# Delta-rule gate projected with tokens on partitions, ahead of the mixer's other projections

## The chip, the cores and the metric

One Trainium2 chip, one of its cores. The metric is the device time of one execution in microseconds; the kernel before has a median of 1240.29 us over three runs (1238.09 to 1243.02).

## The reference, cut to what matters

Two networks follow each other on 256 tokens of width 1024. The first has a Mamba2 layer, an attention layer and two MLPs. The second, where the change lies, has a token mixer of two branches and a mixture of 32 experts. Inside the mixer:

```
proj = h @ w_in            # h is the normed, modulated input
qa, ka, va, qkv_b, z_b, b_b, a_b, gate_a, gate_b = split(proj)
y_a = attention(qa, ka, va)
qkv_b = silu(conv(qkv_b));  beta = sigmoid(b_b);  g = -exp(a_log) * softplus(a_b + dt_bias)
o_b = gated_delta_rule(q_b, k_b, v_b, beta, g)
y_b = rms_norm(o_b, onorm_w) * silu(z_b)          # z_b: 512 columns, the gate
m = sigmoid(gate_a) * (y_a @ w_up_a) + sigmoid(gate_b) * (y_b @ w_up_b)
return m @ w_out
```

## The kernel before, in words

Weights come from HBM as blocks of 128 x 2048 (`wload`, L187, through SyncE's queue into five `wraw` buffers). `split` (L196) cuts a block into two units of 1024 columns and turns each into a high part `whi` (ScalarE, L207) and a low part `wlo` (VectorE, or GpSimd for the units named in `pool`, L208). Both live in the pool `wsp`, which has as many buffers for each of the two as its argument says (L184); in the mixer that is 4, on the right end of SBUF (L909). A product is three matmuls, high x high, high x low, low x high (`mm3`, L235). All matmuls of such products have line L233.

Most projections have features on partitions: `fm` (L240) takes 128 weight columns as the stationary operand and 256 tokens as the moving one, so a block of 256 features is 48 matmuls of 256 columns. The attention values `va` have tokens on partitions: 128 tokens are stationary, 512 weight columns move, 24 matmuls for each of the two token halves (L936 to L942). The gate `z_b` is projected in the first way, two blocks of 256 features, and goes through `silu2` (L321: `th` on ScalarE, `zz` on VectorE).

The mixer's input `hT` is made in the stage before it: `rms_tile` (L880) norms one token half after the other, with its scratch tiles `dg` and `lv` in that stage's pool `mlp`. The last operation of each half is `hTl` (L904). The first half's `hT` is there some 9 us before the second's; the values' matmuls of the first token half stand in between. Every engine takes its instructions in the order that the planner gave them, which follows the order of the code, priorities and the planner's own estimate of when an operand is there.

`branches` (L922) is the mixer. The projections of its first part run in the order of `plan` (L989). From L1214 on a hand-written sequence of the delta rule runs, and `fill()` (L1185) puts units of independent matmuls between its steps: `fillers` (L1160) yields 28 of them, 4 for the gate (24 matmuls each), 16 for the two output gates (24 each) and 8 for `w_upa` (12 each). Between the sixteenth and the eight it loads two expert blocks early. The calls of `fill` from L1214 to L1281 take 24 units, and `fill(40)` (L1296) takes what is left. `dt_chain` (L960) computes the decay `g` and `beta` from `wba` (8 columns of weights, loaded at L944 through ScalarE's queue) and its split `w16`; its `ba` matmuls are the first after the values, and `sums` (L288) with the `csT` transposes follow later.

At the end of the delta rule (L1282 to L1295) the result `po` is scaled into `os_`, transposed (`ot`), multiplied by `onw` and the gate, and split into the two parts of `yb`, on which the `w_upb` products wait (L1299 to L1309, last step `mt` and `ml` on VectorE). Then `mixer_out` (L1312) loads a row `g1`, and SyncE's queue goes on to the expert weights `eraw` (L1537, 1 MB each), in order.

SBUF is laid out by pools, as the sizes in the code give it (bytes per partition). Pools that stay end at 72,320. In the first network `lnp` (17,088) and eight pairs of `wsp` (65,536) reach 154,944; `mlp` stands behind them, with 25,664 bytes of other tiles, then its two `lv` buffers at 180,608 to 184,704. In the mixer `keep` and `mixw` stand on the left and end at 181,760, and the four pairs of `wsp` take the right end from 196,576 to 229,344, `whi` below `wlo`.

Of the kernel before, what the change touches and what calls it, by code (L numbers as in the profile page):

```python
# [10 lines left out]
F32 = mybir.dt.float32  # L11
F32R = mybir.dt.float32r
# [6 lines left out]
T = 256  # L19
# [37 lines left out]
def lay(i):  # L57
# [67 lines left out]
    for n in ("q", "k"):  # L125
# [15 lines left out]
                                                    ("z", 3072, 512), ("g", 3592, 2048))}  # L141
    for n, c in cols.items():
        a["w_b" + n] = fblocks(w, c)
    a["w_bva"] = kblocks(w[:, 1024:1536])
    ba = np.concatenate([w[:, 3588:3592], w[:, 3584:3588]], axis=1)
# [14 lines left out]
def build(tc, A, out, dbg=None):  # L160
# [3 lines left out]
    with ctx:  # L164
# [123 lines left out]
        def sums(work, bank, n, da, ncs, rs):  # L288
            p = bank("cs")
            mm(p[:, 0:n], ic, da[:, 0:n], True, True)  # L290
            mm(p[:, n:2 * n], iu, da[:, n:2 * n], True, True)
            mm(p[:, 2 * n:3 * n], ic, da[:, n:2 * n], True, True)
            mm(p[:, 3 * n:4 * n], su, da[:, 0:n], True, True)
            cs = p[:, 0:3 * n].rearrange("p (b n) -> p b n", b=3)
            csr = work.tile([128, 3, n], F32, name="csr", tag="th")
            V.tensor_copy(csr, cs)
            V.tensor_scalar(ncs, cs[:, 0:3:2], -1.0, None, op0=OP.mult)
            V.tensor_copy(rs, p[:, 3 * n:4 * n])
            p = bank("csT")
            for b in range(3):  # L300
                PE.transpose(p[:n, b * 128:b * 128 + 128], csr[:, b], ident)
            row = work.tile([n, 384], F32, name="csrow", tag="cbm", bufs=2 if n == 32 else 1)
            V.tensor_copy(row, p[:n, 0:384])
            nc.scalar.dma_start(csd[n], row)
# [602 lines left out]
        def phase_mixer(keep, hT):  # L907
            gates = [keep.tile([128, 8, T], F32, name="gates", tag=t) for t in ("gA", "gB")]
            with wsp_pool(4, "right") as w_:  # L909
# [12 lines left out]
        def branches(keep, work, psm, hT, gates):  # L922
# [6 lines left out]
            for tag, n, bufs in (("va", 1024, 1), ("pt", 384, 4), ("s", 384, 3), ("lm", 896, 1), ("cbm", 384, 1), ("bc", 1536, 1), ("ml0", 512, 1),  # L929
                                 ("ml1", 512, 1), ("MT", 1536, 1), ("PT", 1536, 1), ("Tn0", 512, 1), ("Tn1", 512, 1),  # L930
                                 ("X0", 512, 1), ("X1", 512, 1), ("zz", 1024, 1), ("bias", 2048, 1), ("QK", 2048, 1)):
                work.tile([128, n], F32, name=tag, tag=tag, bufs=bufs)
            va = work.tile([128, 2, 512], F32, name="va", tag="va")
            vacc = [pa("va") for _ in range(2)]
            hls = [wsplit(A["w_bva"][b], pool=(0, 1)) for b in range(2)]
            for m in range(2):  # L936
                ms = slice(m * 128, m * 128 + 128)
                for c in range(8):
                    hl = hls[c // 4]
                    wh, wl = (x[:, (c % 2) * 512:(c % 2) * 512 + 512] for x in hl[c % 4 // 2])  # L940
                    mm3(vacc[m], hT[0][:, c, ms], hT[1][:, c, ms], wh, wl, c == 0, c == 7)
                S.activation(va[:, m], vacc[m], AF.Copy)  # L942
            wba = work.tile([128, 8, 8], F32, name="wba", tag="wba")
            nc.scalar.dma_start(wba, A["w_bba"])  # L944
# [11 lines left out]
            w16 = work.tile([128, 8, 16], F32R, name="w16", tag="w16")  # L956
            S.activation(w16[:, :, 0:8], wba, AF.Copy)
            V.tensor_tensor(w16[:, :, 8:16], wba, w16[:, :, 0:8], op=OP.subtract)
# [25 lines left out]
            zz = work.tile([128, 4, T], F32, name="zz", tag="zz")  # L984
# [175 lines left out]
            def fillers():  # L1160
                for b in range(2):
                    for f, p in enumerate(proj2("w_bz", b)):
                        silu2(work, p, zz[:, 2 * b + f])
                        yield
# [86 lines left out]
            def values(b):  # L1251
# [8 lines left out]
                for h in range(4):  # L1260
                    junk = work.tile([128, 128], F32, name="junk", tag="jk", bufs=2)
# [22 lines left out]
            ybt = zz  # L1284
            for b in range(2):
                os_ = work.tile([128, 4, 128], F32, name="os_", tag=f"X{b}")
                V.tensor_tensor(os_, v4(po[b]), ss[:, 1, 4 * b:4 * b + 4].unsqueeze(2).to_broadcast([128, 4, 128]),
                                op=OP.mult)
                p = pa("ot")
# [3 lines left out]
                V.scalar_tensor_tensor(ybt[:, :, bs], v4(p), onw[:, 0:1], zz[:, :, bs], op0=OP.mult, op1=OP.mult)  # L1293
                S.activation(yb[0][:, :, bs], ybt[:, :, bs], AF.Copy)
                V.tensor_tensor(yb[1][:, :, bs], ybt[:, :, bs], yb[0][:, :, bs], op=OP.subtract)  # L1295
# [557 lines left out]
```

## Time and profile before

| | |
|---|---|
| median of three runs | 1240.29 us |
| the profiled execution | 1241.94 us |
| its span, first to last instruction | 1240.2 us |
| mean granted TensorE clock | 0.983 |
| TensorE matmul busy | 1181.6 us (95%) |
| VectorE / ScalarE / GpSimd busy | 757.1 / 554.4 / 215.7 us |

The profile is of one execution. Times in its rows are counted from the first instruction. PE is TensorE's matmul, PEld its weight load, DVE VectorE, ACT ScalarE, POOL GpSimd, SP SyncE; "q" behind an engine is its queue of DMA issues. The granted clock is a share of full speed; 0.50 is 1.2 GHz, 1.00 is 2.4 GHz. The duration of a pipelined matmul overlaps that of the next, so the distance of two starts says what one costs.

### The profile page before, as it was taken

The page shows a single profiled execution, that of the slowest core. Times are in us where ns is not written, and L with a number is a line of the kernel's source. Part 1 is how long each engine was busy: PE and PEld are TensorE (multiplying, and loading weights), DVE is VectorE, ACT ScalarE, POOL GpSimd, SP SyncE. Part 2 cuts the span into 40 slices and gives each one's busy share as a digit, 9 for nine tenths or more (in the row PEclk, how much of TensorE's full clock was granted, in tenths as well). Part 3 has the DMA queues.
Part 4 walks back from the last instruction along what each step waited for, and adds up shares of the span by engine and source line. Part 5 has one row for each costly group of instructions (what it writes and reads, how often), then busy time and mean ns, then how long its engine had stood idle before and what let it go on. Part 6 is the DMA issues. An engine that isn't in the chain of part 4 may idle for free. (4 is left out here: it accounts for less than half of the span.)

```text
span 1240.2 us, 19177 instructions
## 1 busy us (share of the span) xinstructions
PE 1181.6 (95%) x7669; PEld 966.7 (78%) x7669; DVE 757.1 (61%) x1241; ACT 554.4 (45%) x910; POOL 215.7 (17%) x164
## 2 busy tenths in 40 slices
PE   8799996999999999999999998999999989999995
PEld 7799995889899889978999987998999853444332
DVE  5878877497777675559777766667455772111113
ACT  4577573354444455646544434554444431111112
POOL 3355543000000000000000043355431020000001
PEclk9899999999999999999999999899999999999998
DMA  8655634547887744324878753443325599999992
GB/s 325 220 187 196 221 128 146 206 175 282 311 312 285 253 170 170 137 101 158 330 282 300 276 201 118 163 170 103 103 69 204 232 388 407 421 422 421 421 421 108
DMA packets 47078, 295.84 MB, mean 239 GB/s; under 512 B 5256, under 2 KB 6533, under 8 KB 14469
## 3 DMA queue, kind: packets, MB, share of 16 engines
q1 hardware_dynamic: 41120, 277.91, 59.6%
q10 hardware_dynamic: 5860, 16.63, 3.9%
q8 instruction: 62, 1.02, 0.3%
q14 instruction: 36, 0.29, 0.1%
HBM read 293.38 MB, written 2.71 MB: 239 GB/s over the span
## 5 line engine op out<-in xcount | busy, mean ns | idle before, releaser
L208 DVE TENSOR_TENSOR wlo<-wraw,whi 128x1024 fp32r<-128x1024 f32 x240 | 303.1, 1278 | 146.4 <-ACT whi L207 145.5
L207 ACT ACTIVATE whi<-wraw 128x1024 fp32r<-128x1024 f32 x282 | 294.0, 1057 | 212.0 <-PE acc L233 65.4
L208 POOL TENSOR_TENSOR wlo<-wraw,whi 128x1024 fp32r<-128x1024 f32 x42 | 109.8, 2622 | 265.6 <-ACT whi L207 265.6
L233 PE MATMUL u<-hTh,whi 128*128 128x256 f32 x448 | 125.7, 281 | 0.0
L233 PE MATMUL u<-hTh,wlo 128*128 128x256 f32 x448 | 125.3, 280 | 0.0
L233 PE MATMUL u<-hTl,whi 128*128 128x256 f32 x448 | 125.2, 280 | 0.0
L233 PE MATMUL pj<-xh,whi 128*128 128x256 f32 x384 | 113.2, 295 | 6.4 <-ACT whi L387 5.3
L233 PE MATMUL gu<-eraw,xg 128*64 128x512 f32 x512 | 113.3, 595 | 1.1 <-PE xgp L233 0.6
L233 PE MATMUL acc<-whi,mh 128*128 128x512 f32 x288 | 113.8, 395 | 0.0
L233 PE MATMUL pj<-xh,wlo 128*128 128x256 f32 x384 | 110.6, 288 | 3.3 <-DVE wlo L208 3.2
L233 PE MATMUL acc<-whi,ml 128*128 128x512 f32 x288 | 112.7, 391 | 0.0
L233 PE MATMUL acc<-wlo,mh 128*128 128x512 f32 x288 | 112.3, 390 | 0.0
L233 PE MATMUL pj<-xl,whi 128*128 128x256 f32 x384 | 110.8, 289 | 0.3
L233 PE MATMUL pj<-hTh,whi 128*128 128x256 f32 x320 | 93.4, 292 | 0.0
L233 PE MATMUL pj<-hTh,wlo 128*128 128x256 f32 x320 | 91.1, 285 | 0.0
L233 PE MATMUL pj<-hTl,whi 128*128 128x256 f32 x320 | 91.0, 284 | 0.0
L233 PEld LDWEIGHTS gu<-eraw,xg 128*64 128x64 f32 x512 | 36.9, 137 | 66.7 <-issue 62.5
L233 PEld LDWEIGHTS u<-hTh,whi 128*128 128x128 f32 x448 | 84.1, 188 | 1.7 <-issue 0.6
L233 PEld LDWEIGHTS u<-hTl,whi 128*128 128x128 f32 x448 | 83.9, 187 | 1.1
L233 PEld LDWEIGHTS u<-hTh,wlo 128*128 128x128 f32 x448 | 84.4, 188 | 0.0
L233 PEld LDWEIGHTS pj<-xh,whi 128*128 128x128 f32 x384 | 75.3, 196 | 8.8 <-ACT whi L387 5.3
L233 PEld LDWEIGHTS pj<-xh,wlo 128*128 128x128 f32 x384 | 75.5, 197 | 3.9 <-DVE wlo L208 3.4
(450 smaller groups left out, 2386.6 us busy)
## 6 DMA issues: line engine op xcount, KB each, us to landing
wraw<-in_w_dram SPq DMA_DIRECT2D x64, 1024.0 KB, 5.0
eraw<-in_w_gu_dram SPq DMA_DIRECT2D x58, 1024.0 KB, 19.3
eraw<-in_w_dn_dram SPq DMA_DIRECT2D x30, 1024.0 KB, 19.8
wraw<-in_w_mod_dram SPq DMA_DIRECT2D x24, 1024.0 KB, 6.0
wraw<-in_w_a_dram SPq DMA_DIRECT2D x23, 1024.0 KB, 5.3
wraw<-in_w_ao_dram SPq DMA_DIRECT2D x8, 1024.0 KB, 5.0
wraw<-in_w_bg_dram SPq DMA_DIRECT2D x8, 1024.0 KB, 5.1
bc<-csd ACTq DMA_DIRECT2D x16, 384.0 KB, 5.7
```

Of the source, the lines that this page charges most:

```text
L207: his.append(S.activation(h, r[:, us], AF.Copy).ins)
L208: (G if u in pool else V).tensor_tensor(l, r[:, us], h, op=OP.subtract)
L233: return PE.matmul(o, a, b, start=start, stop=stop, skip_group_check=True).ins
```

## The change

The gate's weights get the layout of the values' weights, and its projection moves to the top of `branches`, with tokens on partitions: for each token half the first four of eight weight chunks right behind that half's values, and the last four of both halves after that. `silu2` runs there on token-major rows, so `zz` is [128, 2, 512] from then on. The pool of split weights has 6 pairs instead of 4; to make room `csrow` shares the tag `s`, and `junk` has one buffer. `wba` is loaded first, through SyncE's queue, and `w16` is made between the values' halves. The gate's four units leave `fillers`. At the end, `os_` is multiplied by the gate before the transposes, and `yb` comes straight from the transposed tile.

```
@@ -138,10 +138,11 @@
     a["rel"] = f(i["rel_bias_2"])
     w = f(i["w_in_2"])[0]
     cols = {n: range(c, c + k, 256) for n, c, k in (("qa", 0, 512), ("ka", 512, 512), ("qkv", 1536, 1536),
-                                                    ("z", 3072, 512), ("g", 3592, 2048))}
+                                                    ("g", 3592, 2048))}
     for n, c in cols.items():
         a["w_b" + n] = fblocks(w, c)
     a["w_bva"] = kblocks(w[:, 1024:1536])
+    a["w_bz"] = kblocks(w[:, 3072:3584])
     ba = np.concatenate([w[:, 3588:3592], w[:, 3584:3588]], axis=1)
     a["w_bba"] = np.ascontiguousarray(ba.reshape(8, 128, 8).transpose(1, 0, 2))
     for n in "ab":
@@ -299,7 +300,7 @@
             p = bank("csT")
             for b in range(3):
                 PE.transpose(p[:n, b * 128:b * 128 + 128], csr[:, b], ident)
-            row = work.tile([n, 384], F32, name="csrow", tag="cbm", bufs=2 if n == 32 else 1)
+            row = work.tile([n, 384], F32, name="csrow", tag="cbm" if n == 32 else "s", bufs=2 if n == 32 else 3)
             V.tensor_copy(row, p[:n, 0:384])
             nc.scalar.dma_start(csd[n], row)
 
@@ -906,7 +907,7 @@
 
         def phase_mixer(keep, hT):
             gates = [keep.tile([128, 8, T], F32, name="gates", tag=t) for t in ("gA", "gB")]
-            with wsp_pool(4, "right") as w_:
+            with wsp_pool(6, "right") as w_:
                 wsp_box.append(w_)
                 with tc.tile_pool(name="mixw", bufs=1, reuse_waits="tile") as work, \
                         tc.tile_pool(name="psm", bufs=4, space=PSUM, reuse_waits="tile") as psm:
@@ -926,22 +927,41 @@
             def v4(p):
                 return p.rearrange("p (h n) -> p h n", h=4)
 
-            for tag, n, bufs in (("va", 1024, 1), ("pt", 384, 4), ("s", 384, 3), ("lm", 896, 1), ("cbm", 384, 1), ("bc", 1536, 1), ("ml0", 512, 1),
+            for tag, n, bufs in (("va", 1024, 1), ("pt", 384, 4), ("s", 384, 3), ("lm", 896, 1), ("bc", 1536, 1), ("ml0", 512, 1),
                                  ("ml1", 512, 1), ("MT", 1536, 1), ("PT", 1536, 1), ("Tn0", 512, 1), ("Tn1", 512, 1),
                                  ("X0", 512, 1), ("X1", 512, 1), ("zz", 1024, 1), ("bias", 2048, 1), ("QK", 2048, 1)):
                 work.tile([128, n], F32, name=tag, tag=tag, bufs=bufs)
+            wba = work.tile([128, 8, 8], F32, name="wba", tag="wba")
+            nc.sync.dma_start(wba, A["w_bba"])
+            w16 = work.tile([128, 8, 16], F32R, name="w16", tag="w16")
             va = work.tile([128, 2, 512], F32, name="va", tag="va")
-            vacc = [pa("va") for _ in range(2)]
-            hls = [wsplit(A["w_bva"][b], pool=(0, 1)) for b in range(2)]
+            zz = work.tile([128, 2, 512], F32, name="zz", tag="zz")
+
+            def rows_in(p, hls, m, cs=range(8)):
+                ms = slice(m * 128, m * 128 + 128)
+                for c in cs:
+                    wh, wl = (x[:, (c % 2) * 512:(c % 2) * 512 + 512] for x in hls[c // 4][c % 4 // 2])
+                    mm3(p, hT[0][:, c, ms], hT[1][:, c, ms], wh, wl, c == 0, c == 7)
+
+            def silu_rows(p, m):
+                for n in range(2):
+                    silu2(work, p[:, n * 256:n * 256 + 256], zz[:, m, n * 256:n * 256 + 256])
+
+            hva = [wsplit(A["w_bva"][b], pool=(0, 1)) for b in range(2)]
+            pva, pz = ([pa(n) for _ in range(2)] for n in ("va", "z"))
+            rows_in(pva[0], hva, 0)
+            S.activation(va[:, 0], pva[0], AF.Copy)
+            hz = [wsplit(A["w_bz"][0], pool=(0, 1))]
+            rows_in(pz[0], hz, 0, range(4))
+            S.activation(w16[:, :, 0:8], wba, AF.Copy)
+            V.tensor_tensor(w16[:, :, 8:16], wba, w16[:, :, 0:8], op=OP.subtract)
+            rows_in(pva[1], hva, 1)
+            S.activation(va[:, 1], pva[1], AF.Copy)
+            hz.append(wsplit(A["w_bz"][1], pool=(1,)))
+            rows_in(pz[1], hz, 1, range(4))
             for m in range(2):
-                ms = slice(m * 128, m * 128 + 128)
-                for c in range(8):
-                    hl = hls[c // 4]
-                    wh, wl = (x[:, (c % 2) * 512:(c % 2) * 512 + 512] for x in hl[c % 4 // 2])
-                    mm3(vacc[m], hT[0][:, c, ms], hT[1][:, c, ms], wh, wl, c == 0, c == 7)
-                S.activation(va[:, m], vacc[m], AF.Copy)
-            wba = work.tile([128, 8, 8], F32, name="wba", tag="wba")
-            nc.scalar.dma_start(wba, A["w_bba"])
+                rows_in(pz[m], hz, m, range(4, 8))
+                silu_rows(pz[m], m)
             lm = work.tile([128, 7, 128], F32, name="lm", tag="lm")
             nc.scalar.dma_start(lm, A["lvl"])
 
@@ -953,9 +973,6 @@
             beta = work.tile([128, 2, 4], F32, name="beta", tag="beta")
             onw = work.tile([128, 1], F32, name="onw", tag="onw")
             V.tensor_scalar(onw, P("onw"), 0.5, None, op0=OP.mult)
-            w16 = work.tile([128, 8, 16], F32R, name="w16", tag="w16")
-            S.activation(w16[:, :, 0:8], wba, AF.Copy)
-            V.tensor_tensor(w16[:, :, 8:16], wba, w16[:, :, 0:8], op=OP.subtract)
 
             def dt_chain():
                 p = pst("ba")
@@ -981,7 +998,6 @@
             QK = work.tile([128, 8, T], F32, name="QK", tag="QK")
             vT = keep.tile([128, 2, 2, 4, 128], F32, name="vT", tag="vT")
             vt = vT[:, 0]
-            zz = work.tile([128, 4, T], F32, name="zz", tag="zz")
             qk = keep.tile([128, 2, 4, T], F32, name="qk", tag="qk")
             qa, ka = qk[:, 0], qk[:, 1]
 
@@ -1158,10 +1174,6 @@
             early = []
 
             def fillers():
-                for b in range(2):
-                    for f, p in enumerate(proj2("w_bz", b)):
-                        silu2(work, p, zz[:, 2 * b + f])
-                        yield
                 for b in range(8):
                     for f, p in enumerate(proj2("w_bg", b)):
                         S.activation(gates[b // 4][:, 2 * b % 8 + f], p, AF.Tanh, scale=0.5)
@@ -1258,7 +1270,7 @@
                         mm(o, PT[:, h, 128:256], w[0][:, h], True, False)
                         mm(o, PT[:, h, 256:384], w[1][:, h], False, True)
                 for h in range(4):
-                    junk = work.tile([128, 128], F32, name="junk", tag="jk", bufs=2)
+                    junk = work.tile([128, 128], F32, name="junk", tag="jk", bufs=1)
                     S.activation(junk, v4(po[b])[:, h], AF.Square, accum_out=ss[:, 0, 4 * b + h:4 * b + h + 1])
                 r = slice(4 * b, 4 * b + 4)
                 V.tensor_scalar(ss[:, 1, r], ss[:, 0, r], 1.0 / 128, 1e-6, op0=OP.mult, op1=OP.add)
@@ -1281,18 +1293,18 @@
             fill(2)
             yb2 = keep.tile([128, 2, 4, T], F32R, name="yb", tag="vT")
             yb = [yb2[:, d] for d in range(2)]
-            ybt = zz
             for b in range(2):
                 os_ = work.tile([128, 4, 128], F32, name="os_", tag=f"X{b}")
                 V.tensor_tensor(os_, v4(po[b]), ss[:, 1, 4 * b:4 * b + 4].unsqueeze(2).to_broadcast([128, 4, 128]),
                                 op=OP.mult)
+                V.tensor_tensor(os_, os_, zz[:, b].rearrange("p (h n) -> p h n", h=4), op=OP.mult)
                 p = pa("ot")
                 for h in range(4):
                     PE.transpose(v4(p)[:, h], os_[:, h], ident)
                 bs = slice(b * 128, b * 128 + 128)
-                V.scalar_tensor_tensor(ybt[:, :, bs], v4(p), onw[:, 0:1], zz[:, :, bs], op0=OP.mult, op1=OP.mult)
-                S.activation(yb[0][:, :, bs], ybt[:, :, bs], AF.Copy)
-                V.tensor_tensor(yb[1][:, :, bs], ybt[:, :, bs], yb[0][:, :, bs], op=OP.subtract)
+                S.activation(yb[0][:, :, bs], v4(p), AF.Copy, scale=onw[:, 0:1])
+                V.scalar_tensor_tensor(yb[1][:, :, bs], v4(p), onw[:, 0:1], yb[0][:, :, bs],
+                                       op0=OP.mult, op1=OP.subtract)
             fill(40)
             mh = keep.tile([128, 8, T], F32R, name="mh", tag="gA")
             ml = keep.tile([128, 8, T], F32R, name="ml", tag="qk")
```

## Rows read from the trace of the kernel before

**Rows 1.** The page, busy tenths in 40 equal slices of the span, TensorE and its granted clock

```profile
PE   8799996999999999999999998999999989999995
...
PEclk9899999999999999999999999899999999999998
```

**Rows 2.** Chain of waits (start us, us, what), SyncE's waits, SyncE's timeline

```profile
1100.13 17.20 DMA eraw<-in_w_gu_dram
...
SPq L524 <- DVE mt L1307: 16.2, 1, 16.2
...
973.42 9.58 SPq L1537 DMA_DIRECT2D eraw<-in_w_gu_dram  x10
```

**Rows 3.** Windows: us, busy (x) of PE, PEld, DVE, ACT, POOL; PEclk, DMA share, GB/s

```profile
860.00:945.00 85.00, 85.00 (x732) 81.53 (x731) 42.17 (x93) 39.60 (x93) 31.98 (x17) 1.00 0.26 88
...
1100.00:1200.00 100.00, 98.05 (x458) 38.32 (x458) 16.73 (x31) 12.99 (x27) 1.18 (x2) 0.99 1.01 421
```

**Rows 4.** Timeline of TensorE, 740 to 764 us; in brackets idle before <- releaser

```profile
743.71 0.39 PE L233 MATMUL va<-whi,hTh 128*128 128x512 f32 x1
...
751.32 2.05 PE L233 MATMUL tp<-dg,h 128*128 128x128 f32 x16 [0.97 <-DVE dg L883]
754.40 0.50 PE L233 MATMUL va<-whi,hTh 128*128 128x512 f32 x1 [1.03 <-DVE hTh L901]
...
761.62 0.29 PE L233 MATMUL ba<-hTh,w 128*16 128x256 f32 x1 [1.09 <-DVE w L958]
```

**Rows 5.** The same timeline, first and last of 21 and of 90 products

```profile
755.46 0.40 PE L233 MATMUL va<-whi,hTh 128*128 128x512 f32 x1
...
760.14 0.40 PE L233 MATMUL va<-whi,hTl 128*128 128x512 f32 x1
...
764.62 0.28 PE L233 MATMUL pj<-hTh,whi 128*128 128x256 f32 x1
...
775.18 0.28 PE L233 MATMUL pj<-hTh,wlo 128*128 128x256 f32 x1
```

**Rows 6.** Timelines of VectorE, ScalarE and GpSimd, 700 to 805 us

```profile
755.66 0.69 DVE L904 TENSOR_TENSOR hTl<-lv,hTh 128x512 fp32r<-128x512 f32 x1 [0.60 <-ACT hTh L903]
...
716.64 4.84 ACT L207 ACTIVATE whi<-wraw 128x1024 fp32r<-128x1024 f32 x5
...
717.76 9.11 POOL L208 TENSOR_TENSOR wlo<-wraw,whi 128x1024 fp32r<-128x1024 f32 x3 [2.25 <-ACT whi L207]
...
802.67 2.43 POOL L208 TENSOR_TENSOR wlo<-wraw,whi 128x1024 fp32r<-128x1024 f32 x1 [8.12 <-ACT whi L207]
```

**Rows 7.** TensorE's timeline at 790 and 200 us, and a window between

```profile
790.48 0.49 PE L301 MATMUL csT<-ident,csr 128*4 128x128 f32 x3 [2.51 <-DVE csr L296]
...
792.00:797.00 5.00, 5.00 (x25) 5.00 (x25) 0.00 (x0) 0.10 (x1) 2.37 (x1) 0.50 0.29 72
...
199.95 0.61 PE L233 MATMUL ss<-ones,Zg 128*128 128x1 f32 x4 [3.44 <-POOL Zg L479]
...
201.25 0.63 PE L233 MATMUL acc<-wlo,yh 128*128 128x512 f32 x1
201.68 0.63 PE L233 MATMUL acc<-whi,yl 128*128 128x512 f32 x1
```

**Rows 8.** End of the delta rule: TensorE, VectorE, ScalarE, 953 to 960 us

```profile
953.34 0.66 PE L1291 MATMUL ot<-ident,os__9610 128*128 128x128 f32 x4
...
953.86 1.40 DVE L1293 SCALAR_TENSOR_TENSOR zz<-ot,onw,zz 128x512 f32<-128x512 f32 x2
955.18 1.22 DVE L208 TENSOR_TENSOR wlo<-wraw,whi 128x1024 fp32r<-128x1024 f32 x1
956.31 1.28 DVE L1295 TENSOR_TENSOR yb<-zz,yb 128x512 fp32r<-128x512 f32 x2
...
954.63 1.29 ACT L1294 ACTIVATE yb<-zz 128x512 fp32r<-128x512 f32 x2 [0.80 <-DVE zz L1293]
...
959.46 0.40 PE L233 MATMUL up<-yb,whi 128*128 128x256 f32 x2
```

More of the change, by code (lines that the diff above doesn't have):

```diff
@@ L144, in lay @@
     a["w_bva"] = kblocks(w[:, 1024:1536])
+    a["w_bz"] = kblocks(w[:, 3072:3584])
     ba = np.concatenate([w[:, 3588:3592], w[:, 3584:3588]], axis=1)
@@ L301, in sums @@
                 PE.transpose(p[:n, b * 128:b * 128 + 128], csr[:, b], ident)
-            row = work.tile([n, 384], F32, name="csrow", tag="cbm", bufs=2 if n == 32 else 1)
+            row = work.tile([n, 384], F32, name="csrow", tag="cbm" if n == 32 else "s", bufs=2 if n == 32 else 3)
             V.tensor_copy(row, p[:n, 0:384])
@@ L908, in phase_mixer @@
             gates = [keep.tile([128, 8, T], F32, name="gates", tag=t) for t in ("gA", "gB")]
-            with wsp_pool(4, "right") as w_:
+            with wsp_pool(6, "right") as w_:
                 wsp_box.append(w_)
@@ L927, in v4 @@
                 return p.rearrange("p (h n) -> p h n", h=4)
-            for tag, n, bufs in (("va", 1024, 1), ("pt", 384, 4), ("s", 384, 3), ("lm", 896, 1), ("cbm", 384, 1), ("bc", 1536, 1), ("ml0", 512, 1),
+            for tag, n, bufs in (("va", 1024, 1), ("pt", 384, 4), ("s", 384, 3), ("lm", 896, 1), ("bc", 1536, 1), ("ml0", 512, 1),
                                  ("ml1", 512, 1), ("MT", 1536, 1), ("PT", 1536, 1), ("Tn0", 512, 1), ("Tn1", 512, 1),
@@ L932, in branches, with rows_in, silu_rows @@
                 work.tile([128, n], F32, name=tag, tag=tag, bufs=bufs)
+            wba = work.tile([128, 8, 8], F32, name="wba", tag="wba")
+            nc.sync.dma_start(wba, A["w_bba"])
+            w16 = work.tile([128, 8, 16], F32R, name="w16", tag="w16")
             va = work.tile([128, 2, 512], F32, name="va", tag="va")
-            vacc = [pa("va") for _ in range(2)]
-            hls = [wsplit(A["w_bva"][b], pool=(0, 1)) for b in range(2)]
-            for m in range(2):
[L937 to L944, printed above, removed]
+            zz = work.tile([128, 2, 512], F32, name="zz", tag="zz")
+            def rows_in(p, hls, m, cs=range(8)):
+                ms = slice(m * 128, m * 128 + 128)
+                for c in cs:
+                    wh, wl = (x[:, (c % 2) * 512:(c % 2) * 512 + 512] for x in hls[c // 4][c % 4 // 2])
+                    mm3(p, hT[0][:, c, ms], hT[1][:, c, ms], wh, wl, c == 0, c == 7)
+            def silu_rows(p, m):
+                for n in range(2):
+                    silu2(work, p[:, n * 256:n * 256 + 256], zz[:, m, n * 256:n * 256 + 256])
+            hva = [wsplit(A["w_bva"][b], pool=(0, 1)) for b in range(2)]
+            pva, pz = ([pa(n) for _ in range(2)] for n in ("va", "z"))
+            rows_in(pva[0], hva, 0)
+            S.activation(va[:, 0], pva[0], AF.Copy)
+            hz = [wsplit(A["w_bz"][0], pool=(0, 1))]
+            rows_in(pz[0], hz, 0, range(4))
+            S.activation(w16[:, :, 0:8], wba, AF.Copy)
+            V.tensor_tensor(w16[:, :, 8:16], wba, w16[:, :, 0:8], op=OP.subtract)
+            rows_in(pva[1], hva, 1)
+            S.activation(va[:, 1], pva[1], AF.Copy)
+            hz.append(wsplit(A["w_bz"][1], pool=(1,)))
+            rows_in(pz[1], hz, 1, range(4))
+            for m in range(2):
+                rows_in(pz[m], hz, m, range(4, 8))
+                silu_rows(pz[m], m)
             lm = work.tile([128, 7, 128], F32, name="lm", tag="lm")
@@ L955, in branches @@
             V.tensor_scalar(onw, P("onw"), 0.5, None, op0=OP.mult)
-            w16 = work.tile([128, 8, 16], F32R, name="w16", tag="w16")
-            S.activation(w16[:, :, 0:8], wba, AF.Copy)
-            V.tensor_tensor(w16[:, :, 8:16], wba, w16[:, :, 0:8], op=OP.subtract)
             def dt_chain():
@@ L983, in branches @@
             vt = vT[:, 0]
-            zz = work.tile([128, 4, T], F32, name="zz", tag="zz")
             qk = keep.tile([128, 2, 4, T], F32, name="qk", tag="qk")
@@ L1160, in fillers @@
             def fillers():
[L1161 to L1164, printed above, removed]
                 for b in range(8):
@@ L1260, in values @@
                 for h in range(4):
-                    junk = work.tile([128, 128], F32, name="junk", tag="jk", bufs=2)
+                    junk = work.tile([128, 128], F32, name="junk", tag="jk", bufs=1)
                     S.activation(junk, v4(po[b])[:, h], AF.Square, accum_out=ss[:, 0, 4 * b + h:4 * b + h + 1])
@@ L1288, in branches @@
                                 op=OP.mult)
+                V.tensor_tensor(os_, os_, zz[:, b].rearrange("p (h n) -> p h n", h=4), op=OP.mult)
                 p = pa("ot")
@@ L1292, in branches @@
                 bs = slice(b * 128, b * 128 + 128)
-                V.scalar_tensor_tensor(ybt[:, :, bs], v4(p), onw[:, 0:1], zz[:, :, bs], op0=OP.mult, op1=OP.mult)
-                S.activation(yb[0][:, :, bs], ybt[:, :, bs], AF.Copy)
-                V.tensor_tensor(yb[1][:, :, bs], ybt[:, :, bs], yb[0][:, :, bs], op=OP.subtract)
+                S.activation(yb[0][:, :, bs], v4(p), AF.Copy, scale=onw[:, 0:1])
+                V.scalar_tensor_tensor(yb[1][:, :, bs], v4(p), onw[:, 0:1], yb[0][:, :, bs],
+                                       op0=OP.mult, op1=OP.subtract)
             fill(40)
```

3 lines of the change are left out of this document (1 added, 2 removed).

## The prediction

> **What bounds the kernel now.** I read the page first. TensorE is busy in nearly every slice and its clock dips only where it idled [rows 1]. The end, though, is not TensorE's: from 1100 us the chain of waits is one expert weight load after another, and the DMA share there is 1.01 [rows 2, 3]. So the loads end the run, and their start is the question. The SyncE timeline has the first ten of them at 973.42 us, right behind the gate row `g1`, for which SyncE waited 16.2 us, until the mixer's last `mt` operation had let go of the bytes `g1` gets [rows 2]. Two things follow: whatever moves the end of the mixer moves the end of the kernel one for one, and a tile of a new pool waits for the last reader of the old tile in its bytes. From 860 to 945 us TensorE is busy 85.00 of 85 us [rows 3], so work taken away there is time won, while holes nearer 750 us are the ones the change means to fill: 0.97 us before the norm's `tp` matmuls, 1.03 us behind them, 1.09 us before `ba`, 3.1 us together [rows 4].
>
> **The change, part by part.**
>
> **The matmuls.** The gate needs 96 matmuls of 256 columns today, and 48 of 512 after. At 512 columns 21 rows start between 755.46 and 760.14 us, (760.14 - 755.46) / 20 = 0.234 us apart; at 256 columns 90 rows between 764.62 and 775.18, 10.56 / 89 = 0.119 us apart [rows 5]. So 48 x 0.234 = 11.2 us go in near 750 us and 96 x 0.119 = 11.4 us leave the stretch behind 820 us: -0.2 us. The wider form wins nothing, it only moves. The Trainium skill, page "TensorE: Matmul & The Clock Gate", section "Back-to-back issue gap", gives a sustained 131 ns per matmul at 512 columns; by that the 48 would cost 6.3 us and my total would be 4.9 us lower, but the rows show 0.234 us and decide.
>
> **The splits, where this goes wrong.** To hold the gate's weights beside the values', the pool of split weights goes from four pairs to six and grows downwards by 16,384 bytes. By the tile sizes in the code it then begins at byte 180,192, with `whi` lowest. The previous stage's `lv` tiles, the scratch of the norm, lie at 180,608 to 184,704. The lowest `whi` buffer and 416 bytes of the next overlap them; with four pairs (from 196,576) nothing did. The last reader of `lv` is VectorE's `hTl` of the second token half, 755.66 + 0.69 = 756.35 us [rows 6]. Today the values' four `whi` are made from 716.6 us and their `wlo` by 726.9, long before the norm ends [rows 6]. I take it that the first `whi` gets the lowest buffer and that later tiles of the same tag are not handed out past it; no row shows the second point, so it carries a chance below. Then no split of this stage starts before 756.35. The first matmul needs one `whi` (4.84 / 5 = 0.97 us) and one GpSimd `wlo` (2.43 alone, 3.04 in a run [rows 6]): 756.35 + 0.97 + 2.43 = 759.8, with hand-overs 760.
>
> TensorE meanwhile: today the values start at 743.7 [rows 4] and fill the norm. After, it idles from 743.7 to `tp` at 751.3, 7.6 us; from the end of `tp`, 753.4, to 760 it has only `ba` (16 matmuls of 256 columns, 16 x 0.119 = 1.9 us), 4.7 us idle. New idle 12.3 us against 3.1 us now: **+9.2 us**. What is behind the waiting instruction: on ScalarE the five other `whi`, on GpSimd their `wlo`, on TensorE all of the mixer.
>
> From 760 on a unit of 1,024 weight columns feeds 12 matmuls (both token halves), 12 x 0.234 = 2.8 us, and GpSimd gives one each 2.4 to 3.0 us. If the halves interleave it hides: 0 us, else up to 3 us. The gate's second block puts one `wlo` on VectorE and one on GpSimd, beside matmuls: 0.
>
> **The clock.** After 3.44 us of idle, matmuls of 512 columns start 0.43 us apart instead of 0.234; after the 2.51 us before `csT` the granted clock is 0.50, the 1.2 GHz level, for all of 792 to 797 us [rows 7]. Two idles of 7.6 and 4.7 us bring the same twice: `tp` (2.05 us [rows 4]) takes 0.43 / 0.234 = 1.84 times as long, +1.7 us on the norm's own path; and `ba` with the first eight or so value matmuls loses 8 x 0.2 = 1.6 us. **+3.3 us**, bounds 0 (the clock stays) and 5.
>
> **The fillers.** 28 units cover the waits of the delta rule today; without the gate's four there are 24, and the calls ahead of `fill(40)` are exactly 24. So nothing is left behind the `ot` transposes, where four units of 12 matmuls (5.6 us) cover the way to `yb` now: `ot` at 953.34, ScalarE 954.63, VectorE 956.31, first matmul on `yb` 959.46 [rows 8]. That way gets a multiplication by the gate more (0.64 us, like the subtraction 1.28 / 2 [rows 8]). TensorE, done with `ot` at 953.9, waits until about 956.5, 2.6 us, and `up` on `ya` now follows attention at once, 0.4 more: **+3 us**. Bounds 0, and 5 if both 1.22 us weight subtractions stand in front on VectorE [rows 8].
>
> **Small moves.** The gate's four `th`/`zz` pairs of 256 columns move forward, under matmuls: 0; without that cover at most 0.7 us each on VectorE, what 512 columns take [rows 8], 2.8 us. `wba` goes from ScalarE's queue to SyncE's; what is behind it there are loads whose buffers are full until splits start: 0. The two gate loads pass in front of the projections' on SyncE; those are needed 20 us later than now: 0. `csrow` in an `s` buffer, one `junk` buffer (ScalarE is in order anyway), the new `yb` pair (one operation for one): 0.
>
> **A stall that may go.** Before `csT` TensorE waits 2.51 us for VectorE, and the half clock behind it costs 5 x (1 - 0.234 / 0.43) = 2.3 us [rows 7]. With splits made during the gate's matmuls VectorE may be ahead there: between -4.8 and 0; nearer to neither, I take **-2.4**.
>
> Sum: -0.2 + 9.2 + 0 + 3.3 + 3 - 2.4 = **+12.9 us**. The profiled execution took 1241.94 us (span 1240.2 and 1.74 around it), 1.65 above the median of the runs, 1240.29. 1241.94 + 12.9 - 1.65 = **1253.2 us**. With each bound: +9.2 - 0.2 - 4.8 = +4.2 at best, 9.2 - 0.2 + 3 + 5 + 5 = +22 at worst: 1244.5 to 1262.3.
>
> **The rivals.** *The buffers come free in time* (0.16), the case that is not slower: no overlap counts, or the planner gives the blocked buffer to a later tile. Then 12 gate matmuls (2.8 us) fill two norm holes (-2.0), `ba` waits no more (-1.1), the end still loses 3 and the stall half goes: -0.2 - 3.1 + 3 - 2.4 = -2.7, 1237.6 us; with the bounds 1232 to 1244. For it: ScalarE and GpSimd are free around 725 us. Against: the bytes. It decides from where the first `whi` starts: before 743 us it holds.
>
> *Only the first buffer is held* (0.08): five splits are made early, but matmuls accumulate from the first unit, so the values still wait until 760; only the gate's 12 matmuls (2.8 us) run in the norm. 12.9 - 2.8 = +10.1: 1250.4 us.
>
> *GpSimd in the norm's way* (0.06): buffers free, but the gate's two subtractions (2.4 to 3.0 us each) stand before a power operation of the norm on GpSimd, worth up to 5 us: -2.7 + 5 = +2.3, 1242.6 us. Against: GpSimd idles from 726.9.
>
> **The numbers.** My forecast holds 0.70. Some 0.5% (6.2 us) is what a measurement of this kernel can tell from no change: below 1234.1 faster, above 1246.5 slower. Slower: nearly all of the forecast (0.66) and of the second rival (0.07): 0.73. Within: tails of these (0.05), over half of the first rival (0.09), the third (0.05): 0.19. Faster: the rest of the first rival, 0.08. 1240 to 1260 takes in the forecast but for its tails, the second and third rivals and the upper part of the first: some 0.8. The likeliest case alone is 1244.5 to 1262.3.
>
> **What would show it.** Right: the first `whi` of the values behind `hTl`, after 756 us, no matmul on `va` before `tp`, idle in front of `tp` near 7 us, granted clock 0.50 near 760, projections starting near 785 instead of 763.5, TensorE waiting for `yb` at the end, and the first expert loads some 13 us later. Wrong: `whi` near 717 us and matmuls on `z` between 750 and 755 us.

## The result and the profile after

The changed kernel is slower: 1255.1 us median (1252.77 to 1259.78, six runs) beside 1239.19 us (1236.3 to 1243.53, six runs), a ratio of 1.0129 with a 95% interval of 1.0102 to 1.0156. The forecast was 1253.2 us, the range 1240 to 1260. A ratio in this document compares fast executions alone and is estimated apart from the two medians beside it, so it can differ from their quotient by some 0.2%. The profiled execution is the slowest of the six, 1259.78 us, with a span of 1258.1 us and a mean granted clock of 0.975.

The two profiled executions do not reach the mixer at the same moment: the norm's first `tp` starts at 738.66 us, before at 740.5. So the stage is compared from there. From the first `tp` to the end of the span the kernel before takes 1240.2 - 740.5 = 499.7 us, this one 1258.1 - 738.7 = 519.4 us: 19.7 us more.

The page's busy tenths in 40 slices, TensorE and its granted clock, the counterpart of [rows 1]:

```profile
PE   8799987999999999999999968999999989999995
PEclk9899998999999999999999988999999979999998
```

Slice 24, from 723 to 755 us, was at 9 tenths or more before and is down to 6 tenths; the clock dips in it and in the next. The timeline of ScalarE at the end of the norm shows why:

```profile
754.92 0.63 ACT L904 ACTIVATE hTh<-lv 128x512 fp32r<-128x512 f32 x1
...
756.36 1.06 ACT L208 ACTIVATE whi<-wraw 128x1024 fp32r<-128x1024 f32 x1 [0.71 <-issue]
...
757.32 4.83 ACT L208 ACTIVATE whi<-wraw 128x1024 fp32r<-128x1024 f32 x5
```

VectorE's timeline has the last reader of `lv` right before it:

```profile
755.58 0.69 DVE L905 TENSOR_TENSOR hTl<-lv,hTh 128x512 fp32r<-128x512 f32 x1 [1.41 <-ACT hTh L904]
```

`hTl` ends at 755.58 + 0.69 = 756.27 and the first `whi` starts at 756.36; before, the values' `whi` came from 716.64 on [rows 6]. TensorE's timeline over the norm, the counterpart of [rows 4, 5] (a figure in brackets is the idle time before the row and what ended it):

```profile
749.50 3.78 PE L234 MATMUL tp<-dg,h 128*128 128x128 f32 x16 [7.43 <-DVE dg L884]
757.47 0.79 PE L234 MATMUL va<-whi,hTh 128*128 128x512 f32 x1 [4.18 <-ACT whi L208]
759.90 0.79 PE L234 MATMUL va<-wlo,hTh 128*128 128x512 f32 x1 [1.64 <-POOL wlo L209]
760.49 0.63 PE L234 MATMUL va<-whi,hTl 128*128 128x512 f32 x1
760.92 0.63 PE L234 MATMUL va<-whi,hTh 128*128 128x512 f32 x1
...
764.12 0.39 PE L234 MATMUL va<-whi,hTl 128*128 128x512 f32 x1
764.35 0.40 PE L234 MATMUL va<-whi,hTh 128*128 128x512 f32 x1
...
771.63 0.50 PE L234 MATMUL z<-wlo,hTh 128*128 128x512 f32 x1 [0.67 <-POOL wlo L209]
```

No matmul on `va` or `z` stands between the two `tp` rows of the norm, and four waits take 7.43 + 4.18 + 1.64 + 0.67 = 13.9 us. `tp` takes 3.78 us where it took 2.05, and the values begin 0.43 us apart (760.49, 760.92) and only later 0.23 (764.12, 764.35). The projections start at 787.3 us, 48.6 us behind the first `tp`; before it was 763.5 - 740.5 = 23.0.

At the other end of the mixer, the counterpart of [rows 8]:

```profile
971.03 0.60 PE L1303 MATMUL ot<-ident,os__9615 128*128 128x128 f32 x4
972.80 0.65 PE L1303 MATMUL ot<-ident,os__9625 128*128 128x128 f32 x4 [1.17 <-DVE os__9625 L1300]
974.24 0.74 PE L234 MATMUL up<-yb,whi 128*128 128x256 f32 x4 [0.78 <-ACT yb L1305]
975.59 0.58 PE L234 MATMUL up<-yb,whi 128*128 128x256 f32 x1 [0.61 <-DVE yb L1306]
```

Three waits, 2.6 us, where TensorE had none. Windows show the clock around these holes, one behind `csT` too [rows 7], and the end (columns as in [rows 3]):

```profile
743.00:764.00 21.00, 8.68 (x27) 6.98 (x28) 9.81 (x20) 9.55 (x17) 8.05 (x6) 0.67 0.25 77
814.00:824.00 10.00, 9.76 (x58) 9.74 (x59) 2.68 (x7) 3.19 (x5) 2.38 (x1) 0.66 0.62 228
974.00:980.00 6.00, 5.15 (x28) 4.95 (x29) 2.41 (x6) 0.75 (x3) 0.00 (x0) 0.72 0.99 395
1120.00:1220.00 100.00, 97.82 (x460) 38.70 (x460) 16.72 (x32) 13.09 (x28) 1.18 (x2) 1.00 1.01 421
```

The end is bound by the loads as before, DMA share 1.01. But SyncE's timeline does not look as foretold, beside [rows 2]:

```profile
971.23 0.33 SPq L525 DMA_DIRECT2D g<-modr  x1
971.61 20.02 SPq L1549 DMA_DIRECT2D eraw<-in_w_gu_dram  x10
991.68 29.75 SPq L1549 DMA_DIRECT2D eraw<-in_w_dn_dram  x4
1021.49 0.90 SPq L1549 DMA_DIRECT2D eraw<-in_w_gu_dram  x2
```

The first ten expert loads are issued from 971.61 us, 1.8 us earlier than before, though the mixer ends 17 us later. SyncE's waits in this stretch say what let them go:

```profile
SPq L1549 <- PE acc L234: 18.4, 1, 18.4
SPq L525 <- PE up L234: 15.8, 1, 15.8
SPq L1549 <- DVE ml L1321: 7.0, 1, 7.0
```

`g1` now waits for `up` instead of `mt`, and the loads behind it wait in their turn, for `ml` and 18.4 us for `acc`. The two loads issued in 0.90 us, which came at 1003.59 us before, come at 1021.49, 17.9 us later.

### The profile page after: what moved, and what is told of

It reads as the page before. It is cut to its first block, busy times and chain, and to the rows that moved or that the text cites. A ratio compares the mean times of both kernels' runs of the same rounds, so it can differ in the third digit from the quotient of the medians.

```text
span 1258.1 us, 19081 instructions
## 1 busy us (share of the span) xinstructions
PE 1188.5 (94%) x7621; PEld 971.3 (77%) x7621; DVE 755.2 (60%) x1240; ACT 555.4 (44%) x910; POOL 214.3 (17%) x165
## 5 line engine op out<-in xcount | busy, mean ns | idle before, releaser
L209 DVE TENSOR_TENSOR wlo<-wraw,whi 128x1024 fp32r<-128x1024 f32 x239 | 298.3, 1263 | 148.1 <-ACT whi L208 147.0
L568 POOL TENSOR_TENSOR mv<-mv,nhalf 128x1 f32<-128x1 f32 x8 | 7.6, 948 | 512.9 <-DVE mv L567 512.9
L234 PE MATMUL pj<-hTh,whi 128*128 128x256 f32 x288 | 84.2, 292 | 1.2 <-DVE QK L331 1.2
L234 PE MATMUL pj<-hTl,whi 128*128 128x256 f32 x288 | 82.0, 285 | 0.0
L234 PE MATMUL pj<-hTh,wlo 128*128 128x256 f32 x288 | 82.0, 285 | 0.0
```

The costliest lines, as they stand in the source:

```text
L209: (G if u in pool else V).tensor_tensor(l, r[:, us], h, op=OP.subtract)
L234: return PE.matmul(o, a, b, start=start, stop=stop, skip_group_check=True).ins
L568: pows[m] = G.tensor_tensor(mv[:, 3:4], mv[:, 2:3], nhalf[:, 0:1], op=OP.pow).ins
```

## The experiments

Each distance "behind `tp`" is counted from the first `tp` of the same profile, since the profiles reach it at different times.

### The norm's scratch moved, six pairs kept

```
-            dg = pool.tile([128, 128], F32, name="dg", tag="dg")
+            dg = pool.tile([128, 128], F32, name="dg", tag="dg", bufs=1)
...
-                v = pool.tile([128, 4, 128], F32, name="lv", tag="lv")
+                v = pool.tile([128, 512], F32, name="lv", tag="mr").rearrange("p (c n) -> p c n", c=4)
```

> The changed kernel, six pairs kept, but the norm's scratch lv shares the two buffers of mr (bytes 175,424 to 179,520, last read near 726 us) and dg has one buffer, so nothing the norm reads late lies above byte 180,192. Theory of the bytes (splits wait for lv): the first whi of the values goes back to near 716 us, the values' matmuls start near 742 us, gate matmuls stand in the norm, the projections start near 772 us instead of 787.3; of the 12.5 us (idle 9.2, clock 3.3) nearly all comes back and some of the 3.1 us of norm holes too, while the loss at the end (2.6 us wait for yb and some 2 us of half clock behind it) stays: 1236 to 1244 us. Rival (the splits are late because the gate's loads, wba and GpSimd's six subtractions are in the way, not because of bytes): still a start of whi after 750 us and 1253 to 1258 us.

Measured: 1235.57 us beside 1237.42, ratio 0.9981 (0.9958 to 1.0004), just below the 1236 to 1244 us that I expected. ScalarE's timeline, then TensorE's:

```profile
710.92 6.74 ACT L208 ACTIVATE whi<-wraw 128x1024 fp32r<-128x1024 f32 x7
```

```profile
744.69 0.40 PE L234 MATMUL z<-wlo,hTh 128*128 128x512 f32 x1
745.63 2.05 PE L234 MATMUL tp<-dg,h 128*128 128x128 f32 x16 [0.54 <-DVE dg L884]
747.44 0.48 PE L234 MATMUL z<-whi,hTl 128*128 128x512 f32 x1
```

The splits are early, the gate's matmuls stand on both sides of `tp`, and `tp` is back at 2.05 us. The projections start 766.1 - 734.7 = 31.4 us behind the first `tp` instead of 48.6. Two tiles of scratch, placed lower, are worth 1.0129 / 0.9981 - 1 = 1.5%, or 1.2% by the second measurement of this kernel (further down): the whole loss either way. The rival, which has `wba`, the gate's loads or GpSimd in the way, falls: all of these are still there.

### The kernel before with six pairs and nothing else

```
-            row = work.tile([n, 384], F32, name="csrow", tag="cbm", bufs=2 if n == 32 else 1)
+            row = work.tile([n, 384], F32, name="csrow", tag="cbm" if n == 32 else "s", bufs=2 if n == 32 else 3)
...
-            with wsp_pool(4, "right") as w_:
+            with wsp_pool(6, "right") as w_:
...
-                    junk = work.tile([128, 128], F32, name="junk", tag="jk", bufs=2)
+                    junk = work.tile([128, 128], F32, name="junk", tag="jk", bufs=1)
```

> The kernel before, feature-major gate in its old place, with nothing but six pairs of split weights (and the two small tiles that make room). Theory of the bytes: whi after 756 us as in the changed kernel, +9.2 idle and +3.3 clock, no loss at the end since the 28 filler units are there: 1248 to 1255 us. Rival (the gate's new place and form cost the time, the number of pairs is harmless): 1236 to 1243 us.

Measured: 1253.09 us beside 1237.42, ratio 1.012 (1.0069 to 1.0172). TensorE's timeline:

```profile
743.82 3.78 PE L233 MATMUL tp<-dg,h 128*128 128x128 f32 x16 [7.43 <-DVE dg L883]
751.79 1.22 PE L233 MATMUL va<-whi,hTh 128*128 128x512 f32 x2 [4.18 <-ACT whi L207]
754.23 0.79 PE L233 MATMUL va<-wlo,hTh 128*128 128x512 f32 x1 [1.23 <-POOL wlo L208]
```

The same holes to a hundredth, 7.43 and 4.18 us, with the gate in its old place and form. The size of the pool alone makes the loss: 1.2% of 1237.42 is 14.8 us, of which the prediction had 12.5. That the two small edits for the room have no part in it is shown below.

### The same with five pairs, and with the room alone

The edit is the one above with `wsp_pool(5, "right")`, so that the pool begins above `lv`.

> The same edit with five pairs: the pool of splits then begins at byte 188,384, above lv's end at 184,704. Theory of the bytes: no wait, whi near 716 us, 1236 to 1242 us. Rival (each further pair costs something, or the two small tiles that make room do): between the kernel before and the one with six pairs, 1243 us or more.

Measured: 1242.3 us, ratio 1.0026 (0.9998 to 1.0054). In its tile view the values and projections start as before, 738.9 and 758.7 us, that is 3.2 and 23.0 us behind `tp`:

```profile
L233 PE MATMUL va<-whi,hTh x16: 388/398/497, 738.9 to 754.9; 128*128 128x512 f32 x16
L233 PE MATMUL pj<-hTh,whi x320: 277/281/581, 758.7 to 946.4; 128*128 128x256 f32 x160
```

So the splits wait for nothing, as the theory of the bytes has it. The time was just above what it expected, so the four-pair kernel with the two small edits was run too (the edit above without its line on the pool):

> The kernel before with four pairs and only the two small edits that make room (csrow shares the tag s, junk has one buffer). e3_before_five_pairs came out at a ratio of 1.0026, open whether the fifth pair or these edits do that. If the edits do (junk in one buffer makes ScalarE wait, csrow waits for an s buffer): ratio 1.002 to 1.003. If the fifth pair does, by another order of the splits: ratio 0.999 to 1.001.

Measured: 1236.66 us beside 1239.47, ratio 0.9982 (0.9958 to 1.0006). The two small edits cost nothing; the ratio lies just below both expectations. What the fifth pair costs, if it does (the intervals just meet), stays open: its profile has a wait of 2.1 us for `Tn` ahead of `X` that the others lack, but no run isolated it.

This run settles another point. With nothing but these edits `g1` is loaded at 958.92 us, 11 us ahead of the first `acc` at 970.0; in the kernel before it came 2.3 us behind it (973.04 and 970.7). SyncE's waits from 940 to 1010 us name the releaser of the changed kernel, `up`:

```profile
SPq L1537 <- PE acc L233: 12.2, 1, 12.2
...
SPq L524 <- PE up L233: 3.2, 1, 3.2
```

By the tile sizes in the code, the room makes `mixw`'s tiles behind `cbm` begin 1,536 bytes lower. Before, the lowest 896 bytes of `g1` lay on the tile `ma`, which `mt` reads; now `g1` lies wholly on `ya`, which `up` reads.

### Four pairs, the gate behind the values

```
-            with wsp_pool(6, "right") as w_:
+            with wsp_pool(4, "right") as w_:
...
-            hz = [wsplit(A["w_bz"][0], pool=(0, 1))]
-            rows_in(pz[0], hz, 0, range(4))
...
-            hz.append(wsplit(A["w_bz"][1], pool=(1,)))
-            rows_in(pz[1], hz, 1, range(4))
+            hz = [wsplit(A["w_bz"][b], pool=(1,)) for b in range(2)]
             for m in range(2):
-                rows_in(pz[m], hz, m, range(4, 8))
+                rows_in(pz[m], hz, m)
                 silu_rows(pz[m], m)
```

> The changed kernel with four pairs again; the gate still has tokens on partitions and stands at the top, but all its 48 matmuls follow the values' (four pairs cannot hold both), so none is in the norm. Theory of the bytes: whi near 716 us, projections start near 763.5 + 11.2 = 775 us, the end loses some 2.6 us of wait and 2 us of clock, the norm's holes stay: 1240 to 1247 us. Rival (the token-major gate and the missing filler units are what costs): near 1255 us.

Measured: 1240.74 us, ratio 1.0019 (0.9995 to 1.0042). The projections start 773.9 - 738.5 = 35.4 us behind `tp`, 12.4 more than before for a gate of 11.2. With tokens on partitions but no gate matmul in the norm, the change would cost 2.4 us; with them there (the scratch moved) the ratio is 0.0038 lower, 4.7 us, or 3.3 us by the mean of that kernel's two measurements (the second is below). The second alone gives 1.9 us, which is within the noise of the two ratios. The profiles agree with the larger figures: with the scratch moved the projections start 31.4 us behind `tp` instead of 35.4. So filling the holes seems to win about their size of 3.1 us; the times alone do not show how much.

### One small scratch tile in the way

As the first experiment, but `dg` keeps its two buffers.

> The kernel with the norm's scratch lv moved, but dg with its two buffers again: the second dg lies at bytes 180,096 to 180,608 and so covers 416 bytes of the lowest whi buffer and no other buffer of the splits. It tells apart whether one held buffer holds all splits. Theory (the first tile gets the lowest buffer, later ones are not handed out past it): all six whi start only after the last tp matmul of the norm, near tp's end (748 to 752 us), TensorE idles ahead of tp as in the changed kernel: 1248 to 1254 us. Rival (only the first buffer is held): five whi are made near 716 us and only the first unit's is late; gate or value matmuls can still not start before it, but ScalarE and GpSimd have the rest ready: 1244 to 1249 us. Second rival (416 bytes of a scratch that small do not matter): as e1_scratch_moved, 1233 to 1238 us.

Measured: 1256.66 us beside 1239.47, ratio 1.016 (1.0122 to 1.0199), as slow as the changed kernel and above the 1248 to 1254 us that I expected. ScalarE's timeline:

```profile
752.12 0.63 ACT L904 ACTIVATE hTh<-lv 128x512 fp32r<-128x512 f32 x1
753.51 0.20 ACT L284 ACTIVATE ac<-pv 128x4 f32<-128x4 f32 x1 [0.76 <-DVE hTl L905]
753.62 1.04 ACT L208 ACTIVATE whi<-wraw 128x1024 fp32r<-128x1024 f32 x1
754.56 4.83 ACT L208 ACTIVATE whi<-wraw 128x1024 fp32r<-128x1024 f32 x5
```

416 bytes on the lowest buffer hold back all six splits, five of which have bytes that were free long before. The rival in which only the first is held falls, and so does the one in which so few bytes don't matter. The start is later than I expected, 753.6 us where `tp` ends near 750.4: the six stand behind the norm's `lv` and `hTh`, which ScalarE has first in its order. The program that this kernel builds has a fixed buffer for each split: the first gets the lowest, the other five those from the top down, none of which `dg` touches. So it is ScalarE's order that holds the five behind the first; a run with another order was not made.

### The units behind the transposes

First the kernel before, with the gate's four units called at once, so that none is left at the end:

```
-            fill()
+            fill(5)
             vturn()
```

> The kernel before with its gate feature-major and four pairs, but four filler units (the gate's) called at once at the first fill, so that none is left behind the ot transposes. It prices the missing fillers alone, without the new form or place of the gate. Theory of the fillers: first matmul on yb waits some 2 us longer (before it is never waited for), some 1 to 2 us of half clock behind: 2 to 4 us more than the kernel before, ratio 1.0015 to 1.0035. Rival (the units behind ot hide nothing that matters): ratio 0.999 to 1.001.

Measured: 1243.25 us beside 1239.47, ratio 1.005 (1.002 to 1.0079), more than either theory had. TensorE's timeline:

```profile
959.07 0.73 PE L233 MATMUL up<-yb,whi 128*128 128x256 f32 x4 [1.98 <-ACT yb L1294]
960.75 0.58 PE L233 MATMUL up<-yb,whi 128*128 128x256 f32 x1 [0.94 <-DVE yb L1295]
```

The waits are 2.9 us. From the first matmul on `yb` to the first `acc` it is 973.2 - 959.1 = 14.1 us instead of 11.2; of these 2.9 us more, 0.9 is the second wait and 2.0 the half clock at which the matmuls begin. Together 4.9 us.

Then the other way: the kernel with the scratch moved, two calls of `fill` left out of the levels, so that two units stand behind `ot`:

```
                 next(at, 0)
-                fill()
+                if lv < 5:
+                    fill()
                 for d in range(2):
                     level_t(lv, d)
```

> The kernel with the norm's scratch moved (e1_scratch_moved), with two calls of fill in the last two levels of the delta rule left out, so that two units of 12 matmuls on ya (2.8 us) stand behind the ot transposes. Theory of the fillers (their lack cost 2.6 us of wait for yb and some 1.6 to 2 us of half clock behind it): the waits for ot and yb shrink to 0.5 us or less, no half clock behind 955 us, and the levels, where TensorE was busy without a gap, give no more than 1 us back: 2 to 4 us less than e1_scratch_moved, 1231 to 1234 us. Rival (TensorE only idles as long in the levels instead): no difference, 1234 to 1238 us.

Measured: 1234.44 us beside 1239.47, ratio 0.9974 (0.9952 to 0.9996). Both waits for `yb` are gone from its profile and one of 1.05 us before `ot` is left. By the ratios this is only 0.9 us better than the first experiment, within the noise, and the time lies in the range of the rival, 1234 to 1238 us, just above that of the theory. So both ran again on one chip, with a third that keeps four units back (`lv < 3`):

> The same kernel as e1_scratch_moved, beside the next two on one chip, so that the worth of units behind the ot transposes is read among them. Theory of the fillers: 2 to 4 us above e10_two_units_again. Rival: within 1 us of it. Either way 0.996 to 1.000 of the kernel before.

> The same kernel as e5_two_units_kept_back. e5 had shown no wait for yb and no half clock behind it in its profile, but timed only 0.9 us below e1_scratch_moved by the ratios. Theory of the fillers: ratio 0.994 to 0.997. Rival (the wait moved elsewhere): 0.997 to 0.999.

> The same with four calls of fill left out of the last four levels, so four units of 12 matmuls (5.6 us) stand behind the ot transposes, as in the kernel before. Theory of the fillers: the way to yb was already covered by two, so no more than 0.5 us is won, and each unit taken out of a level now risks a gap of up to 1 us there: within 2 us of e10_two_units_again. Rival (cover was still short): another 1 to 2 us less.

Measured: 1.0004 (0.998 to 1.0027), 0.9978 (0.9958 to 0.9999) and 0.9994 (0.9972 to 1.0016). The medians are 1238.70, 1235.09 and 1238.12 us. Two units are worth 0.0026 or 3.2 us this time (twelve executions each, on one chip), 2.1 us over both pairs, at the low end of what I expected. The ratio with two units, 0.9978, lies above its 0.994 to 0.997 and in the range of the rival, in which the wait only moves elsewhere; no such wait shows in the profile, where TensorE has no gap in the levels. The scratch moved, at 1.0004, came out just above its range too. Four units give back what two win: 3.0 us more than with two, where I expected no more than 2. The window from 860 to 945 us, with two units kept back and with four:

```profile
860.00:945.00 85.00, 85.00 (x724) 81.41 (x723) 47.17 (x101) 39.82 (x96) 25.00 (x14) 0.99 0.28 100
```

```profile
860.00:945.00 85.00, 83.51 (x703) 79.07 (x702) 49.59 (x102) 37.82 (x90) 26.57 (x16) 0.98 0.26 90
```

With four gone, the levels have 1.5 us of gaps; with two they have none. The kernel with the scratch moved and two units kept back is the best seen: 0.9974 and 0.9978 of the kernel before, some 3 us, in two measurements that both exclude 1, though barely.

## Why the prediction was right, point by point

**The splits wait for the last reader of `lv`: right.** It is shown from three sides: moving the scratch undoes it, six pairs alone make it, five pairs don't. The prediction had whi after 756.35, no value before `tp`, 7.6 and 4.7 us of idle; it was 756.36, none, 7.43 and 4.18. `ba` did not fill the hole behind `tp`, as the prediction had it; it came at 765.16 us, since the split of its weights stands on ScalarE behind the six `whi`, at 762.05 us.

**GpSimd's pace, taken as 0 with a bound of 3: undersized.** TensorE waits 1.64 and 0.67 us for `wlo`. New idle time is 13.9 - 3.1 = 10.8 us instead of 9.2. The 3.1 leaves out a fourth hole, which the kernel before has ahead of the third matmul on `va`:

```profile
744.94 0.49 PE L233 MATMUL va<-whi,hTl 128*128 128x512 f32 x1 [0.61 <-POOL hTl L904]
```

With it the holes to be filled were 3.7 us, the term should have been 8.6, and 10.2 is what came.

**The clock, +3.3: right.** `tp` lost 3.78 - 2.05 = 1.7 us, as worked out, and some ten matmuls of the values, at a granted clock of 0.50 from 757.4 to 763.5 us, 0.2 us each, 2 us. With the idle time that is 14.5, and with the gate's 11.2 it makes 25.7 us; the projections start 48.6 - 23.0 = 25.6 us later. What is left out is small: the hole of 0.61 us above, and `baT`, whose 0.3 us now stand before the projections. The prediction's "near 785" for that start was 2 us below its own terms (763.5 + 11.2 + 12.5 = 787.2).

**The matmuls, -0.2: right.** The gate at the top takes what its rows said: in the changed kernel too, matmuls of 512 columns at full clock start 0.23 us apart. Behind them the way from the first projection to the first `acc` is 200.8 us instead of 207.2, 6.4 less: to within 0.3 the 11.4 that left, but for the 4.7 lost at the end. The 131 ns of the Trainium skill, page "TensorE: Matmul & The Clock Gate", section "Back-to-back issue gap", by which the total would have been 4.9 us lower, does not hold for these rows.

**The fillers, +3: right in kind, too small.** The waits are the 2.6 us foretold. Behind them `up` on `yb` takes 988.1 - 974.2 = 13.9 us instead of 11.2, of which 0.6 is one of the waits and 2.1 half clock, which the sum had only in its bound of 5. The run that takes the units out of the kernel before gives 4.9 us in its profile and 6.2 by its ratio (2.5 to 9.8 by the interval).

**The stall before `csT`, -2.4: wrong.** It is still there, with a clock of 0.66 from 814 to 824 us. TensorE's row, then VectorE's timeline up to the operands of `csT`:

```profile
814.24 0.49 PE L302 MATMUL csT<-ident,csr 128*4 128x128 f32 x3 [1.83 <-DVE rs L299]
```

```profile
812.33 1.22 DVE L209 TENSOR_TENSOR wlo<-wraw,whi 128x1024 fp32r<-128x1024 f32 x1
813.46 0.42 DVE L325 SCALAR_TENSOR_TENSOR QK<-th,QK 128x256 f32<-128x256 f32 x1
813.92 0.17 DVE L297 COPY csr<-cs 128x12 f32<-128x12 f32 x1
```

I had let half of it go because splits might be made earlier. But `csr` stands on VectorE behind a `wlo` and a step on `QK`, as before (788.67 and 789.80 us), though the sums that it copies were there by 806.7 us; these steps moved along with the rest. The wait is 0.7 us shorter, and one of 1.19 us for `QK` before it, at 799.94 us, is new.

**The first expert loads some 13 us later: wrong as a sign, right in what it was for.** The loads that the prediction looked at came 1.8 us earlier, because the room moved the tiles under `g1` by 1,536 bytes, so that it no longer lies on bytes that `mt` reads. I had asked which bytes the splits lie on, and did not ask it of `g1`, whose wait I took as fixed. The early start gained next to nothing, as the next slots wait for `ml` and `acc`. The rule "whatever moves the end of the mixer moves the end one for one" held to within 2 us in every profile: from the first `acc` to the end of the span it is 269.5 us before and 270.0 after, and between 267.7 and 271.3 in all the experiments, while the first `acc` lies anywhere from 961.2 to 988.1 us.

**The sum.** -0.2 + 10.8 + 3.7 + 4.7 = 19.0 us of the 19.7 that the profile shows from the first `tp` (18.4 with the fourth hole). The profiled run stands 4.68 us above its median, the one before 2.75 above the median of its six runs: 19.7 - 1.9 = 17.8. The other 1.8 us to the 15.9 between the medians is the time by which the profiled run reached the norm earlier. The +12.9 forecast is short of the 19.0 by GpSimd's pace (1.6), the clock in the norm (0.4), the half clock at the end (1.7) and what was given back for `csT` (2.4). Between the medians it is 3.0 us short. That the time itself is only 1.9 us off is in part luck: the kernel before came out 1.1 us faster in these runs (1239.19 for 1240.29).

**The rivals.** "The buffers come free in time" is what the first experiment built: 1235.57 us beside 1237.42, where the rival had -2.7, and 1.0004 in its second measurement. "Only the first buffer is held" fell with the experiment on `dg`. GpSimd stood in no one's way in the norm: with the splits made early again the second `tp` follows the first by 745.63 - 734.74 = 10.9 us, as before.

## What to carry to other kernels

A pool that grows takes bytes, and a tile's wait is set by whoever read those bytes last: before one buffer is added, see which tiles lie under the new ones and when they are read. A scratch that covered 416 bytes of one buffer cost as much here as all of the norm's, and moving it cost nothing. Work that looks like filler has to be counted up to its end: two units of 1.4 us behind the last transposes were worth more than the same two in a stretch without gaps, and four won nothing. Compare stages from a common row in both profiles, since the executions reach the stage some microseconds apart.

## What the runs showed of the hardware

The same holes can have two outcomes. The kernel with two units kept back was profiled twice. Ahead of the first `X` TensorE has the same three holes in both, 0.42, 0.57 and 1.20 us, and here are the rows of the last, first from e5_two_units_kept_back, then from e10_two_units_again, the same program:

```profile
858.35 2.38 PE L234 MATMUL X<-Tn,ml 128*128 128x128 f32 x16 [1.20 <-POOL ml L1088]
```

```profile
858.66 3.68 PE L234 MATMUL X<-Tn,ml 128*128 128x128 f32 x16 [1.20 <-POOL ml L1088]
```

Sixteen matmuls of 128 columns took 2.38 us in one execution, at a granted clock of 1.00 over the 3.5 us from there, and 3.68 in the other, at 0.51, the 1.2 GHz level. The kernel before has 2.38 in its profile; the one with the room alone, with the same holes but for 0.05 us, has 3.60. Ten profiles have this row behind a wait of 1.2 us: it takes 2.38 us in three and 3.49 to 3.79 in seven. So three short holes, 2.2 us together, may or may not be followed by the lower clock, in one and the same program. The Trainium skill, page "TensorE: Matmul & The Clock Gate", section "What's actually happening", says that the number of slow matmuls after a start differs from run to run of one kernel; these rows, which follow a hole and not a start, agree in that they differ too. The 7.4 to 7.5 us hole ahead of `tp` was followed by the lower clock, 0.50 through `tp`, in all three profiles that have it. So a short hole is to be priced as a chance of the lower clock and not as a sure loss. Executions of one kernel lie 8 us apart in twelve of e5_two_units_kept_back (1230.14 to 1237.86 us) and 14 us in 29 of the kernel before (1232.17 to 1246.37, beside the last three experiments). The mean granted clock goes with the time: of these 29, the eight at 0.983 or more have a mean of 1235.3 us, the six at 0.978 or less 1241.9. No run isolated the clock's part.
